# Squares added up on POOL, ScalarE or VectorE, spreads by transposes, two partial sums in layer 1, in a decoder trunk of two layers

## The chip, the core and the metric

The kernel runs on one core of one Trainium2 chip. The metric is the time of one execution on the device, in microseconds (us). The core's engines are TensorE (PE in the rows, its weight loads PEld), VectorE (DVE), ScalarE (ACT), GpSimd (POOL) and SyncE (SP), which here issues nearly all DMAs. Each engine works through its own queue in order.

## What is computed

```python
for l in range(DEPTH):                       # 2 layers, 256 tokens, 1024 channels, float32
    h = rmsnorm(x, norm_mix[l])
    (u_ssm, q_lat, kv_lat, k_rope, hg_q, hg_f, hg_i, hg_g, gate_logits) = jnp.split(h @ w_in[l], split_at, axis=-1)
    y_ssm = s5_mixer(u_ssm, ...)             # diagonal complex recurrence
    y_mla = mla_mixer(q_lat, kv_lat, k_rope, ...)   # rmsnorm of q_lat and kv_lat, 8 heads
    y_hg = hgrn2_mixer(hg_q, hg_f, hg_i, hg_g, ...) # gated linear recurrence, rmsnorm of each head
    merged = gates[:, :, 0] * y_ssm + gates[:, :, 1] * y_mla + gates[:, :, 2] * y_hg
    x = x + merged @ w_out[l]
    x = x + memory_cross_attention(rmsnorm(x, norm_cross[l]), rmsnorm(mem, norm_mem[l]), ...)
    x = x + swiglu_ffn(rmsnorm(x, norm_ffn[l]), ffn_w_gate_up[l], ffn_w_down[l])
return rmsnorm(x, norm_final)
```

Every rmsnorm needs the mean of the squares of a token's channels.

## The kernel before

Activations lie with channels on the partitions: x is four tiles xp of 128 partitions by 2 channel blocks by 256 tokens. Weights are loaded by SP in chunks of 1 MB (tile raw, three buffers), and ACT and DVE split each of a chunk's two halves (a unit) into a high part wH and a low part wL in the reduced float32 format fp32r; the normalised operand x is split in the same way into a pair. A product is then three matmuls, high with high, high with low, low with high. `mm3` (L403) makes them in one of two forms. With 256 columns of output these are three matmuls of 256 columns that all add into one half of a PSUM bank. With 512 columns one matmul multiplies the high weights with both parts of x at once, which gives two partial sums side by side in one bank, and a second one of 256 columns adds the third product; someone must then add the two partial sums:

```python
if o.shape[1] == 512:
    mm(o, w[0], x.rearrange("p s t -> p (s t)"), start=first, stop=False)
    mm(o[:, 256:512], w[1], x[:, 0], start=False, stop=last)
```

`pair` (L420) projects 256 output channels into one bank by the first form, `halves` (L427) into two banks by the second, `quad` (L434) 512 channels into four banks by either, and `add_up` (L447) adds two partial sums, by a copy on ACT and an add on DVE for each bank. In both layers the cross attention and the feed-forward part (tiles hv, quad, fa, fu) use the second form. The first projections of a layer (u by `quad`; hf, hq, hg, ql and kv by `pair`) use the first form; their PSUM tiles are named quad, hf and acc.

**Norms.** `Norm.add` squares x by ACT and adds the four squares on DVE to one tile acc of 2 blocks by 256 tokens. `col_sums` (L563) sums that over the partitions on PE: for each half of the tokens (tt_) and each block one matmul of the squares (as the weights) with a column of ones, into a tile ms. A float32 matmul stands as two instructions in the rows. In layer 0's first norm each of the four squares is summed so on its own, by `first` (L624), between the matmuls of u. `mem_norm` (L1129) does the same for the memory, and the tile lat holds the sums for the norms of q_lat and kv_lat. POOL takes the power -1/2 (`rsqrt`, L239). `row_of` (L613) spreads the resulting column, one number per token, over all partitions: a matmul of the broadcast column with the unit matrix `ident`, then a copy by ACT (tiles R, Rkv, Rm). `hgrn` (L962) spreads its eight columns into tiles ro in the same way.

**What sets the order.** The program is written as one main sequence (the projections) and tasks (generators: the recurrences s5 and hgrn, the attention, the memory), of which `pace` (L262) runs a step whenever the planner's own clocks say that DVE and ACT have room. `step` (L250) marks a task as not to be taken up again before its operations are done by these clocks plus a gap, `LATS`, one number per layer. Then a scheduler with a model of the engines orders each engine's queue; `high_priority` moves a piece ahead. `Plan` (L105) gives each tile a buffer of its kind (t4 of 16 KB, t2, t1 and smaller) from a first pass over the program.

In the s5 task (`s5_main`, two halves per layer) PE transposes Gp into PSUM tiles gt, ACT copies these to G, PE makes tm, then b from G, DVE and POOL run the recurrence, PE makes y, SP moves the result ysh by 16 small DMAs into yc, ACT and DVE split it into yx, which is the operand of the last branch (zg, zo). The attention task makes S, PT and oT; mo and ho project the other two branches. A name gt stands for the gates' matmuls as well (with wH and wL).

## Time and profile before

| what | value |
|---|---|
| three runs | 1100.15, 1101.13, 1104.74 us; median 1101.13 |
| the profiled execution | 1100.18 us, of which span 1098.4 us |
| PE busy | 1083.1 us, 6704 matmuls |
| DVE, ACT, POOL busy | 821.5, 641.1, 23.9 us |
| mean granted clock of PE | 0.994 |
| read from memory | 173 MB |

The profile is of one execution. The span runs from its first to its last instruction, and the run's time holds some 1.8 us more around it. A busy time is the sum of an engine's instructions. Matmuls are pipelined, so the duration of one is longer than the distance to the next start. A wait stands for the idle time of an engine just before an instruction, with what ended it.

### The profile page before, as it was taken

To read this page: it belongs to the slowest core of one execution; us is meant where nothing else is said; L and a number is where in the kernel's file an instruction comes from. 1 tells how busy PE (TensorE), PEld (TensorE's weight loads), DVE (VectorE), ACT (ScalarE), POOL (GpSimd) and SP (SyncE) were. 2 spreads that over 40 slices of the span, in tenths; PEclk is the share of its full clock that TensorE was granted. 3 is DMA by queue.
4 is the path that set the end of the run, shared out by engine and by line. 5 is a ranking of instruction groups with operands and counts; after the bars stand their busy time and mean duration, and the time that the engine had idled before them with its cause. 6 is when DMAs were issued, how large, how long until landed. Compare 5 with 4: busy or idle time off the path is not lost.

```text
span 1098.4 us, 17246 instructions
## 1 busy us (share of the span) xinstructions
PE 1083.1 (99%) x6704; PEld 960.9 (87%) x6704; DVE 821.5 (75%) x1415; ACT 641.1 (58%) x1050; POOL 23.9 (2%) x44
## 2 busy tenths in 40 slices
PE   9999999999999999999999999999999999999997
PEld 9999888887788888888899999888878888888887
DVE  7996877587586799986767877658677767877653
ACT  6647565954456566555555348775555566655552
POOL 1000000000000000000000001000000000000000
PEclk9999999999999999999999999999999999999999
DMA  9735523323644465655655443434474534655561
GB/s 312 214 110 183 175 96 120 123 93 112 223 154 154 154 197 178 198 183 169 206 176 150 123 133 125 154 115 153 133 241 154 192 115 155 206 182 186 173 199 50
DMA packets 146306, 177.69 MB, mean 162 GB/s; under 512 B 15153, under 2 KB 110385, under 8 KB 146225
## 3 DMA queue, kind: packets, MB, share of 16 engines
q1 hardware_dynamic: 145792, 176.03, 49.9%
q8 instruction: 52, 0.85, 0.3%
q10 hardware_dynamic: 432, 0.57, 0.2%
q14 instruction: 30, 0.24, 0.1%
HBM read 173.43 MB, written 1.05 MB: 159 GB/s over the span
## 4 chain that ended last, share of the span: by engine, by line
PE 92%; ACT 3%; DVE 1%; DMA 1%; issue 1%; SPq 0%; POOLq 0%; POOL 0%; ACTq 0%; DVEq 0%
PE hv L204 27%; PE dn L204 11%; PE gt L204 11%; PE acc L204 8%; PE quad L204 7%; PE vps L204 2%; PE lv L204 2%; PE mo L204 2%; PE xv L204 2%; PE y L204 2%; PE zg L204 2%; PE hf L204 2%; PE zo L204 2%; PE b L204 1%; PE q L204 1%; ACT wH L223 1%
## 5 line engine op out<-in xcount | busy, mean ns | idle before, releaser
L223 ACT ACTIVATE wH<-raw 128x1024 fp32r<-128x1024 f32 (+2 forms) x332 | 341.2, 1032 | 318.4 <-PE hv L204 66.9
L212 DVE TENSOR_TENSOR wL<-raw,wH 128x1024 fp32r<-128x1024 f32 (+2 forms) x332 | 393.7, 1189 | 172.2 <-ACT wH L223 167.6
L204 PE MATMUL hv<-h,wH 128*128 128x512 f32 x704 | 247.0, 396 | 0.0
L204 PE MATMUL hv<-h,wL 128*128 128x256 f32 x704 | 195.9, 281 | 0.0
L204 PEld LDWEIGHTS hv<-h,wH 128*128 128x128 f32 x704 | 131.4, 188 | 30.5
L204 PEld LDWEIGHTS hv<-h,wL 128*128 128x128 f32 x704 | 132.9, 189 | 0.9
L204 PE MATMUL gt<-wH,h 128*128 128x512 f32 x384 | 123.9, 402 | 0.0
L204 PE MATMUL acc<-h,wH 128*128 128x256 f32 x480 | 88.8, 285 | 0.0
L204 PEld LDWEIGHTS gt<-wH,h 128*128 128x128 f32 x384 | 70.5, 189 | 13.3
L204 PE MATMUL gt<-wL,h 128*128 128x512 f32 x192 | 75.6, 395 | 0.0
L204 PEld LDWEIGHTS acc<-h,wH 128*128 128x128 f32 x480 | 75.0, 191 | 0.4
L204 PE MATMUL acc<-h,wL 128*128 128x256 f32 x240 | 68.0, 283 | 0.0
L204 PE MATMUL dn<-dx,wH 128*128 128x512 f32 x176 | 61.8, 394 | 0.0
L204 PE MATMUL dn<-wH,dx 128*128 128x256 f32 (+1 forms) x264 | 58.8, 319 | 0.0
L204 PE MATMUL dn<-dx,wL 128*128 128x256 f32 x176 | 49.4, 281 | 0.0
L204 PEld LDWEIGHTS dn<-wH,dx 128*128 128x128 f32 x264 | 43.6, 189 | 4.0
L204 PEld LDWEIGHTS acc<-h,wL 128*128 128x128 f32 x240 | 45.9, 191 | 0.0
L204 PE MATMUL quad<-h,wH 128*128 128x256 f32 (+1 forms) x192 | 45.4, 323 | 0.2 <-ACT wH L223 0.2
L204 PEld LDWEIGHTS gt<-wL,h 128*128 128x128 f32 x192 | 36.0, 188 | 7.6
L204 PE MATMUL dn<-wL,dx 128*128 128x256 f32 (+1 forms) x132 | 41.9, 319 | 0.0
L204 PEld LDWEIGHTS dn<-dx,wH 128*128 128x128 f32 x176 | 33.1, 188 | 7.8
L204 PEld LDWEIGHTS quad<-h,wH 128*128 128x128 f32 x192 | 30.9, 190 | 3.2 <-ACT wH L223 0.5
(362 smaller groups left out, 2093.7 us busy)
## 6 DMA issues: line engine op xcount, KB each, us to landing
raw<-in_w_in_dram SPq DMA_DIRECT2D x48, 1024.0 KB, 5.2
raw<-in_ffn_w_gate_up_dram SPq DMA_DIRECT2D x40, 1024.0 KB, 5.1
raw<-in_ffn_w_down_dram SPq DMA_DIRECT2D x17, 1024.0 KB, 5.2
raw<-in_ssm_w_glu_dram SPq DMA_DIRECT2D x16, 512.0 KB, 4.3
raw<-in_w_out_dram SPq DMA_DIRECT2D x8, 1024.0 KB, 7.3
raw<-in_x_w_kv_dram SPq DMA_DIRECT2D x8, 1024.0 KB, 5.2
raw<-in_ffn_w_down_dram SPq DMA_DIRECT2D x6, 768.0 KB, 4.5
raw<-in_hg_w_o_dram SPq DMA_DIRECT2D x4, 1024.0 KB, 5.0
```

The source lines that it names most:

```text
L204: return PE.matmul(o, l, r, start=start, stop=stop)
L212: DVE.tensor_tensor(out=o, in0=a, in1=b, op=op)
L223: return ACT.activation(out=o, in_=a, func=f, **kw)
```

## The change

1. The squares are added up before PE sums them. `fold` adds the two channel blocks of a square, on DVE or POOL, and `col_sums` is left with one matmul for each half of the tokens. In layer 0's first norm POOL adds the four squares as they come and folds the result, and PE sums once. For q_lat the add of two squares moves from DVE to POOL, with the fold.
2. The memory's norm is taken from a second copy of the memory with tokens on the partitions (`mem_rows`, 1 MB more to load), by two ACT squares that also accumulate; `mem_norm` and its sums on PE are gone.
3. `wide_col` spreads a column by a PE transpose in place of a float32 matmul, in `row_of` and for ro.
4. In layer 1 u, hf, hq, hg, ql and kv are made as two partial sums (`halves`, and `quad` with n=512) and added by `add_up`.
5. The planner: `LATS` (0.9, 1.7) in place of (1.1, 2.2); a task can ask for more time at a yield (2.0 us after the move to yc, 1.5 us after the power function in hgrn); small tiles may take a larger buffer where their kind is full.

The diff, with unchanged lines left out:

```diff
--- before
+++ after
@@ -80,6 +80,7 @@
         o[n] = c(v[n].reshape(T, KD, 128).transpose(2, 1, 0))
+    o["mem_rows"] = v["mem"].reshape(T, DM)
     o["gains"] = c(np.concatenate([v[n].reshape(-1, 128) for n, _ in GAINS]).T)
@@ -96,7 +97,7 @@
 LEAD = 2
-LATS = (1.1,2.2)
+LATS = (0.9, 1.7)
 WIDE = 2
@@ -121,17 +122,21 @@
-                e = ends[kind]
-                h = min(range(len(e)), key=lambda q: e[q])
-                if e[h] >= first:
-                    raise MemoryError(f"no home for tile {i}, {kind}")
-                e[h] = last
-                self.homes[i] = h
+
+                for k in dict(t1=("t1", "t2", "t4"), t2=("t2", "t4")).get(kind, (kind,)):
+                    e = ends[k]
+                    h = min(range(len(e)), key=lambda q: e[q])
+                    if e[h] < first:
+                        e[h] = last
+                        self.homes[i] = f"{k}_{h}"
+                        break
+                else:
+                    raise MemoryError(f"no home for tile {i}, {kind}, at {first}")
...
-        t_ = pool.tile(shape, dt, tag=f"{kind}_{i if self.homes is None else self.homes[i]}", name=name)
+        t_ = pool.tile(shape, dt, tag=self.homes[i] if self.homes else f"{kind}_{i}", name=name)
@@ -249,14 +254,16 @@
 
+
         was = dict(now)
+        more = 0.0
         try:
-            next(e[0])
+            more = next(e[0]) or 0.0
         except StopIteration:
...
         if moved:
-            e[1] = max(moved + [now["pe"]]) + gap_[0]
+            e[1] = max(moved + [now["pe"]]) + gap_[0] + more
         return bool(moved)
@@ -560,17 +567,19 @@
 
-    def col_sums(sqs, ps=None, first=True, last=True, pin=False):
+    def fold(s, E=None):
+
+        if E is not None:
+            E.tensor_tensor(out=s[:, 0], in0=s[:, 0], in1=s[:, 1], op=ALU.add)
+        else:
+            tt(s[:, 0], s[:, 0], s[:, 1], ALU.add)
+        return s[:, 0]
+
+    def col_sums(s, ps=None):
 
         ps = ps if ps is not None else bank("ms")[:, 0:2]
-        for n, s in enumerate(sqs):
-            for tt_ in range(2):
-                for o in range(2):
-
-                    m = mm(ps[:, tt_:tt_ + 1], s[:, o, tt_ * 128:tt_ * 128 + 128], ones,
-                           start=first and n + o + tt_ == 0, stop=last and n == len(sqs) - 1 and o + tt_ == 2)
-                    if pin:
-                        tc.keep_in_program_order(m)
+        for tt_ in range(2):
+            mm(ps[:, tt_:tt_ + 1], s[:, tt_ * 128:tt_ * 128 + 128], ones)
         return ps
@@ -603,19 +612,24 @@
             if self.sums is None:
-                self.sums = col_sums([self.acc])
+                self.sums = col_sums(fold(self.acc))
             ms = tk([2])
...
 
+    def wide_col(o, col):
+
+        now["pe"] += 0.11
+        PE.transpose(o, col.to_broadcast([128, 128]), ident)
+
     def row_of(col, o):
...
             for tt_ in range(2):
-                mm(ps[:, tt_ * 128:(tt_ + 1) * 128], col[:, tt_:tt_ + 1].to_broadcast([128, 128]), ident)
+                wide_col(ps[:, tt_ * 128:(tt_ + 1) * 128], col[:, tt_:tt_ + 1])
             acopy(o, ps[:, 0:256])
@@ -637,8 +651,10 @@
             sq0.append(s)
-        if k > 3:
-            nrm.sums = col_sums(sq0[k - 4:k - 3], nrm.sums, k == 4, k == 7, True)
+            if j:
+                POOL.tensor_tensor(out=sq0[0], in0=sq0[0], in1=s, op=ALU.add)
+            if j == 3:
+                fold(sq0[0], POOL)
 
@@ -948,7 +964,7 @@
                     SP.dma_start(out=yc[32 * c_:32 * c_ + 32, :, j, :], in_=ysh[32 * j:32 * j + 32, c_::4, :])
-            yield
+            yield 2.0
             yx = t4([2, 2, 256], F32R, "yx")
@@ -1045,14 +1061,14 @@
         rsqrt(ro, mo)
-        yield
+        yield 1.5
         for hp in range(2):
...
                     c_ = 2 * (2 * hp + o) + tt_
-                    mm(rp[:, 256 * o + 128 * tt_:256 * o + 128 * tt_ + 128], ro[:, c_:c_ + 1].to_broadcast([128, 128]), ident)
+                    wide_col(rp[:, 256 * o + 128 * tt_:256 * o + 128 * tt_ + 128], ro[:, c_:c_ + 1])
             ov = osb[:, 2 * hp:2 * hp + 2]
@@ -1124,18 +1140,16 @@
             memT.extend(m4[:, j] for j in range(2))
+        nat = [t4([1024], F32, "mnat") for _ in range(2)]
+        for tt_ in range(2):
+            SP.dma_start(out=nat[tt_], in_=A["mem_rows"][128 * tt_:128 * tt_ + 128])
         yield
 
-    def mem_norm():
-
-        ps = None
-        for j in range(4):
-            s = t2([2, 256], F32, "sqm")
-            act(s, memT[j], AF.Square)
-            ps = col_sums([s], ps, j == 0, j == 3)
-            yield
-        ms = tn([2])
-        ts(ms, ps, 1.0 / DM, EPS, ALU.mult, ALU.add)
+        junk, msq, ms = t4([1024], F32, "junk"), tn([2]), tn([2])
+        for tt_ in range(2):
+            act(junk, nat[tt_], AF.Square, accum_out=msq[:, tt_:tt_ + 1])
+            yield
+        ts(ms, msq, 1.0 / DM, EPS, ALU.mult, ALU.add)
         rsqrt(rmc, ms)
@@ -1148,8 +1162,6 @@
             yield
-        if l == 0:
-            yield from mem_norm()
 
@@ -1170,12 +1182,36 @@
         Ue = t4([4, 4, 64], F32, "Ue")
-        qp = quad(C["u"], hx, first if l == 0 else None)
+        wider = l > 0
+
+        def scaled(a, c):
+
+            if wider:
+                add_up(a, halves(c, hx))
+                tt(a, a, Rp, ALU.mult)
+            else:
+                tt(a, pair(c, hx), Rp, ALU.mult)
+
+        def two_tiles(c):
+            if not wider:
+                return pair(c, hx)
+            a = t2([2, 256], F32, "lt")
+            add_up(a, halves(c, hx))
+            return a
+
+        qp = quad(C["u"], hx, first if l == 0 else None, 512 if wider else 256)
+        if l == 0:
+            nrm.sums = col_sums(sq0[0][:, 0])
         ms, r = nrm.finish()
...
         with tc.high_priority(offset=HP):
+            if wider:
+                us = [t2([2, 256], F32, "us") for _ in range(2)]
+                for q in range(2):
+                    add_up(us[q], qp[2 * q:2 * q + 2])
+                qp = [us[o // 2][:, o % 2] for o in range(4)]
             for o in range(4):
@@ -1191,18 +1227,16 @@
         for i in range(2):
-            ps = pair(C["hf"][i], hx, ps=mbank("hf") if i < (2, 1)[l] else None)
             a = t2([2, 256], F32, "a")
-            tt(a, ps, Rp, ALU.mult)
+            scaled(a, C["hf"][i])
             act(a, a, AF.Tanh, scale=0.5)
...
         for i in range(2):
-            ps = pair(C["hq"][i], hx)
             a, tq = t2([2, 256], F32, "a"), t2([2, 256], F32, "tq")
-            tt(a, ps, Rp, ALU.mult)
+            scaled(a, C["hq"][i])
             act(tq, a, AF.Tanh, scale=0.5)
@@ -1216,9 +1250,8 @@
         for i in range(2):
-            ps = pair(C["hg"][i], hx)
             a, tq = t2([2, 256], F32, "a"), t2([2, 256], F32, "tq")
-            tt(a, ps, Rp, ALU.mult)
+            scaled(a, C["hg"][i])
             act(tq, a, AF.Tanh, scale=0.5)
@@ -1226,7 +1259,7 @@
         for i in range(2):
-            ps = pair(C["ql"][i], hx)
+            ps = two_tiles(C["ql"][i])
             s = t2([2, 256], F32, "sqq")
@@ -1235,8 +1268,9 @@
                 split_g(qx[:, o, 0], qx[:, o, 1], ps[:, o], gain("mla_q_norm", 4 * l + k))
-        tt(sq2[0], sq2[0], sq2[1], ALU.add)
-        ps = pair(C["kv"], hx)
+        POOL.tensor_tensor(out=sq2[0], in0=sq2[0], in1=sq2[1], op=ALU.add)
+        fold(sq2[0], POOL)
+        ps = two_tiles(C["kv"])
         skv = t2([2, 256], F32, "skv")
@@ -1256,10 +1290,9 @@
         lps = sbank("lat")
+        fold(skv)
         for n, s in ((0, sq2[0]), (1, skv)):
-            for tt_ in range(2):
-                for o in range(2):
-                    mm(lps[:, 2 * n + tt_:2 * n + tt_ + 1], s[:, o, tt_ * 128:tt_ * 128 + 128], ones, start=o == 0, stop=o == 1)
+            col_sums(s[:, 0], lps[:, 2 * n:2 * n + 2])
         me, lat, rl = tn([2]), tn([4]), tn([4])
```

The sequence on the engines changes with it. Three places, as the queues stand before and after; a number behind a name is the tile's, and the rows of the changed kernel have the line numbers of its own file.

PE in layer 0's first stage, where quad is the projection u, h the operand, ms the sums and row the spread. Before, near the end of the sums (four are in the row, each two instructions):

```order
L204 MATMUL quad_135<-h_115,wL_170 128x256
L204 MATMUL ms_247<-ones,sq_268 128x1 x4
L204 MATMUL quad_132<-h_116,wH_175 128x256 x2
L204 MATMUL quad_132<-h_116,wL_176 128x256
L204 MATMUL quad_133<-h_116,wH_175 128x256 x2
```

and with the change:

```order
L209 MATMUL quad_135<-h_116,wH_175 128x256 x2
L209 MATMUL ms_317<-ones,sq_193 128x1 x2
L209 MATMUL quad_132<-h_116,wL_176 128x256
L209 MATMUL quad_133<-h_116,wL_176 128x256
L209 MATMUL quad_134<-h_116,wL_176 128x256
```

Four rows of sums between the matmuls of u became one, 80 matmuls into u, and the fifth row block of u follows the fourth directly.

POOL from the start of the program, where A and Vp are tiles of zeros, n is the norm's power function and rh half of it. Before:

```order
L1295 MEMSET Vp_1322 128x1024
L241 ISA
L241 TENSOR_TENSOR n_332<-n_330,mhalf 128x2
L1213 TENSOR_SCALAR rh_716<-n_332 128x2
L862 MEMSET rt_1756 128x8
```

and with the change:

```order
L1328 MEMSET Vp_1305 128x1024
L655 ISA
L655 TENSOR_TENSOR sq_193<-sq_193,sq_229 128x512
L655 TENSOR_TENSOR sq_193<-sq_193,sq_264 128x512
L655 TENSOR_TENSOR sq_193<-sq_193,sq_301 128x512
L573 TENSOR_TENSOR sq_193<-sq_193 128x256
L246 TENSOR_TENSOR n_322<-n_320,mhalf 128x2
```

Three adds and the fold stand ahead of the power function that the first spread needs.

PE at the second half of layer 0's s5 task. Before:

```order
L869 MATMUL gt_2384<-ident,Gp_2285 128x128 x4
L869 MATMUL gt_2356<-ident,Gp_2284 128x128 x4
L204 MATMUL tm_2424<-Pw_961,Gp_2284 32x64
...
L204 MATMUL S_2694<-Kh_1312,Qh_1310 128x256
L204 MATMUL b_2462<-Ush_343,G_2348 128x64 x4
L204 MATMUL b_2463<-Ush_343,G_2349 128x64 x4
L1071 MATMUL PT_2449<-ident,Ssb_2296 128x128 x3
```

and with the change:

```order
L885 MATMUL gt_2429<-ident,Gp_2330 128x128 x4
L209 MATMUL tm_2465<-Pw_1097,Gp_2330 32x64
...
L209 MATMUL S_2490<-Kh_1295,Qh_1293 128x256
L209 MATMUL gt_2415<-wH_2318,h_113 128x512 x2
L209 MATMUL gt_2415<-wL_2319,h_113 128x512
L209 MATMUL b_2510<-Ush_333,G_2388 128x64 x8
L209 MATMUL b_2511<-Ush_333,G_2389 128x64 x8
```

One group of transposes is left in front of tm; three gate matmuls stand between S and b, and all eight of the first b come ahead of the second. Some way behind, 12 matmuls of mo stand ahead of y's main group, where 7 stood before.

## Rows read from the trace of the kernel before

**Rows 1.** The page's busy times: us (share of span) xinstructions.

```profile
PE 1083.1 (99%) x6704; PEld 960.9 (87%) x6704; DVE 821.5 (75%) x1415; ACT 641.1 (58%) x1050; POOL 23.9 (2%) x44
```

**Rows 2.** Waits of PE: tile <- what it waited for: us, times, longest.

```profile
PE mT L1375 <- DVE Tg L212: 1.9, 1, 1.9
PE mo L204 <- ACT Tg L223: 1.2, 1, 1.2
PE b L204 <- ACT G L223: 1.2, 1, 1.2
PE zg L204 <- DVE yx L212: 0.9, 1, 0.9
```

**Rows 3.** Stretches, layer 0: us, PE PEld DVE ACT POOL busy, clock, DMA, GB/s.

```profile
215.00:220.00 5.00, 3.80 (x25) 3.40 (x24) 2.73 (x5) 4.97 (x10) 0.00 (x0) 0.82 0.75 256
220.00:225.00 5.00, 5.00 (x24) 4.82 (x24) 4.57 (x11) 3.63 (x10) 0.11 (x1) 0.50 0.75 272
286.00:290.00 4.00, 3.19 (x12) 2.86 (x13) 3.84 (x7) 0.00 (x0) 0.00 (x0) 0.57 0.37 123
```

**Rows 4.** Chain that ended last, first 60 us: start us, us, what.

```profile
6.81 6.01 PE quad L204 x48
12.82 0.79 PE ms L204 x8
...
24.16 0.45 PE row L204 x4
...
34.09 11.52 PE acc L204 x96
```

**Rows 5.** Chain that ended last: two later pieces.

```profile
390.61 104.18 PE hv L204 x597
...
685.95 1.78 PE ro L204 x16
```

**Rows 6.** Groups by line, PE: shapes | busy us, mean ns | idle before.

```profile
L204 PE MATMUL ms<-ones,sq 128*128 128x1 f32 x72 | 8.5, 240 | 0.0
...
L204 PE MATMUL ms<-ones,sqm 128*128 128x1 f32 x32 | 3.7, 245 | 0.0
...
L204 PE MATMUL row<-ident,n 128*128 128x128 f32 x16 | 2.4, 274 | 0.0
...
L204 PE MATMUL lat<-ones,skv 128*128 128x1 f32 x16 | 1.9, 239 | 0.0
```

**Rows 7.** Timeline of PE at transposes: start us, us, instructions.

```profile
211.82 1.04 PE L869 MATMUL gt<-ident,Gp 128*128 128x128 f32 x8
212.78 1.97 PE L204 MATMUL tm<-Pw,Gp 128*32 128x64 f32 x32
```

**Rows 8.** Groups by line, PE: transposes of one kind.

```profile
L869 PE MATMUL gt<-ident,Gp 128*128 128x128 f32 x64 | 8.6, 272 | 0.0
```

**Rows 9.** Groups by line, ACT and DVE, in the feed-forward part.

```profile
L223 ACT ACTIVATE fa<-hv 128x256 f32<-128x256 f32 x40 | 14.6, 366 | 0.0
...
L212 DVE TENSOR_TENSOR fa<-fa,hv 128x256 f32<-128x256 f32 x40 | 16.5, 413 | 0.0
```

**Rows 10.** Stretches of layer 1's projections and of the feed-forward part.

```profile
570.00:590.00 20.00, 20.00 (x186) 19.78 (x186) 12.09 (x18) 14.73 (x22) 0.72 (x2) 1.00 0.40 101
600.00:610.00 10.00, 10.00 (x49) 8.39 (x49) 10.00 (x15) 4.49 (x5) 0.11 (x1) 1.00 0.55 173
400.00:450.00 50.00, 50.00 (x287) 43.59 (x287) 48.85 (x90) 30.89 (x50) 0.00 (x0) 1.00 0.59 195
```

**Rows 11.** Timeline of ACT in the first stage.

```profile
12.19 2.18 ACT L223 ACTIVATE wH<-raw 128x512 fp32r<-128x512 f32 x4
```

**Rows 12.** Timeline of POOL.

```profile
0.76 0.95 POOL L966 MEMSET A<- 128x1024 f32 x1
...
171.38 1.64 POOL L241 TENSOR_TENSOR s<-s,mhalf 128x8 f32<-128x8 f32 x1 [5.43 <-DVE s L219]
```

**Rows 13.** Timeline of PE before the last branch of layer 0.

```profile
265.53 0.50 PE L204 MATMUL zg<-wH,yx 128*128 128x512 f32 x1 [0.90 <-DVE yx L212]
```

## The prediction, made before the run

> **What bounds the kernel now.** I read the engines' busy shares first [rows 1]: TensorE (PE) is busy for 1083.1 of the 1098.4 us of the span, VectorE (DVE) and ScalarE (ACT) for three quarters and for less than two thirds. A busy PE can be a PE that idles inside long matmuls, so I read next what PE waited for [rows 2]: its four longest waits are of 1.9, 1.2, 1.2 and 0.9 us, all in layer 0 between 215 and 287 us, and they are nearly all that there is once the matmuls have begun. Then the granted clock of that stretch [rows 3]: after the wait of 1.2 us at 215 us the clock is at its lower level (1.2 in place of 2.4 GHz) for 36% of 215 to 220 us and all of 220 to 225, and after the wait of 1.9 us at 285 us for 86% of 286 to 290; at the lower level work takes twice as long, so these cost 0.9 + 2.5 + 1.7 = 5.1 us. Waits and clock together are 5.2 + 5.1 = 10.3 us. Everywhere else matmul follows matmul. So the kernel is bound by the number of matmuls times the distance from one start to the next, and this distance, not the duration of one matmul, is the price of everything that the change takes from PE. Distances I take from the chain that ended last, where PE's pieces follow each other without a gap [rows 4, 5].
>
> **The sums on PE.** A float32 matmul stands as two instructions in the rows. Column sums (tiles ms and lat) are 72 + 32 + 16 + 16 instructions [rows 6] (lat has two groups alike, one of which stands there). After the change layer 0's first norm keeps 4 of its 32, the five other norms keep 4 of 8 each, the memory's 32 go altogether, lat keeps 16 of 32: 24 + 0 + 16 = 40 are left, 96 go. Eight of them take 0.79 us in the chain [rows 4], 0.099 us each: **-9.5 us**.
>
> **The spreads.** A column is spread by 64 matmul instructions now: 16 in row for the norms [rows 6] and two rows of 8 like it, 16 in ro in each layer [rows 5]. Four take 0.45 us [rows 4], sixteen 1.78 us [rows 5], so 0.112 us each, 7.2 us together. A transpose of 128x128 is one instruction: eight follow each other from 211.82 us until the next group starts at 212.78 [rows 7], 0.12 us each. 32 of them cost 3.8 us: **-3.3 us** (the two ends of the new price are 0.12, the distance, and 0.272, the duration of one [rows 8], as if none overlapped; I take 0.12, since PE does start the next one that soon). TensorE: Matmul & The Clock Gate in the Trainium skill (Part 4: PE-mode transpose) gives about 275 ns for a transpose in a kernel's context; the duration in the trace agrees, the distance does not, and by the page's price this term would be +1.6 us in place of -3.3.
>
> **The second layer's projections.** As one sum a 256-column chunk is 48 matmuls of 256 columns; 96 take 11.52 us [rows 4], 0.120 each, 5.76 a chunk. As two sums it is 16 of 512 and 16 of 256; 597 such take 104.18 us [rows 5], 0.1745 each, 5.58 a chunk. Nine chunks save 0.18 each, the u projection (96 to 64 matmuls) 11.52 - 11.17 = 0.35: **-1.9 us**.
>
> **What the other engines get.** Each of the nine pairs, and u as two more, gains two ACT copies of 256 columns and two DVE adds (0.366 and 0.413 us) [rows 9], the multiplication by R staying one of 512: 22 of each, 8.1 us of ACT and 9.1 of DVE, over the 90 us of layer 1's projections. I cost it at nothing: from 400 to 450 us, where all chunks are made this way, DVE is busy 48.85 of 50 us and PE never idles [rows 10]. The cover is thinner from 600 to 610 us, where DVE already is busy 10.00 of 10 us with the recurrence's steps [rows 10]; that is the first rival. Seven halving adds of 256 columns come to DVE (five norms, lat's second sum in each layer), 0.4 us each: PE's sums stand behind them in its queue, but only after many more matmuls of the projection under way than these 0.4 us. In return the add of the two lat squares leaves DVE for POOL, which is nearly idle. The memory's rows, 1 MB more to load, go out on SP ahead of the last branch's weights; SP has no other load to make there, since each of these waits for a raw buffer, and ACT's squares of them take the place of four others.
>
> **POOL in the first stage.** The new order puts the two sums after 80 matmuls of u, and PE works in order, so a late POOL stops PE there. PE starts at 6.81 us and reaches that place at 6.81 + 80 x 0.12 = 16.4 us. The last square is done when ACT turns to its four weight pieces at 12.19 us [rows 11]. Behind it stand one POOL add of 512 and one of 256 columns. The trace has no such add. From below: a POOL memset of 1024 columns takes 0.95 us [rows 12], 0.48 for 512, as if reading were free. From above: the power function on 8 columns takes 1.64 us [rows 12], 0.2 us a column, 105 us for 512. I take 1.4 us (two reads and a write, each as dear as the memset's write), far nearer to the memset, since an add is no power function; 1.5 x 1.4 = 2.1 us end at 14.3 us, 2 us before PE asks. GPSIMD Engine Reference in the Trainium skill (4.1 Engine selection) says to leave two-input elementwise work to VectorE, being about twice as slow on POOL, and its 4497 ns for 2048 columns make an estimate of 1.1 us; the sum would be the same. What PE meets there instead: with no sums between, it wants the weights of the fifth row block at 6.81 + 48 x 0.12 = 12.6 us, and ACT has the first piece (a quarter of 2.18 us [rows 11]) at 12.75: +0.2 us.
>
> **The moved waits.** Before b (layer 0, second half) PE sends both its last groups of transposes, tm and S, then waits 1.2 us for ACT's copies [rows 2]. In the new order one group goes far earlier, and between the last and the first b that needs it stand gate matmuls and 8 of b: -1.2 us. Before the second zg group PE waits 0.9 us for yx, behind the move of y through SP [rows 13]; now 12 in place of 7 mo matmuls stand ahead of y, so 5 of 512 columns fewer lie behind it, at (5.58 - 16 x 0.12) / 16 = 0.23 us from the chunk above: +1.2 us. The two that remain, mo and mT, I leave as they are; the shorter gap of the planner (0.9 and 1.7 us) can move them either way.
>
> Sum: -9.5 - 3.3 - 1.9 = -14.7; + 0.2 - 1.2 + 1.2 = **-14.5 us**. The profiled execution took 1100.2 us, 0.9 under the median of the three runs and beside their fastest. **1085.7 us**.
>
> **Rivals.**
> 1. DVE becomes the bound in layer 1's projections. For it: 10.00 of 10 us at 600 us. Against: from 570 to 590 us, where u and both hf pairs fall (four of the eleven), DVE is busy 12.09 of 20 us [rows 10] and takes its share. If all that is added for the other seven came back as waits, 14 x 0.413 = 5.8 us: 1091.5.
> 2. In-order waits take over, and it gets slower. With gaps of 1.1 us layer 0 has its four waits, each with its share of the lower clock 10.3 / 4 = 2.6 us; layer 1, with 2.2, has none. The change shortens both gaps and speeds PE up against DVE and ACT. If layer 0 gets four more and layer 1 as many as that, +20.6 us: 1106.3. It decides from six such waits on (14.5 / 2.6). Against: the special waits behind the SP move and the power function, and the order, in which the producers of layer 1 stand well ahead.
> 3. What PE loses was filler: sums and spreads come out, and PE waits that long at the next operand instead; the change then does not do what it says: 1100. Against: no wait of PE stands anywhere near most of these instructions [rows 2].
> 4. A transpose costs its duration: 32 x (0.272 - 0.12) = +4.9, 1090.6. The page named above has that price; the trace speaks against it [rows 7, 8].
> 5. POOL adds at the power function's rate: three and a half adds of 105 us, some 1450. Only the far bound speaks for it.
>
> **Chances.** Forecast 0.70 (its own range 1080 to 1091: the lower clock gone, or two more waits of 2.6 us), rival 1 0.10, rival 2 0.06, rival 3 0.07, rival 4 0.04, rival 5 0.03. A difference of 0.5%, 5.5 us, is what a measurement of this kernel can tell. Faster by more: 0.70 + 0.10 + 0.04 = 0.84; within: 0.07; slower: 0.06 + 0.03 = 0.09. The range reaches down to 1078 (the 5.1 us of lower clock gone, and mT's wait of 1.9 too: 1078.7) and up to 1094, past rivals 1 and 4.
>
> **What would show it.** PE matmul instructions fall by 96 + 32 + 9 x 16 + 32 = 304, from 6704 to 6400. First stage: sums at about 16.4 us without a wait, the first pair of projections at 6.81 + 96 x 0.12 + 0.4 + 0.2 = 18.9 us. Row and ro groups at half their length. Layer 1: 32 matmuls a chunk in 5.6 us, and DVE above nine tenths from 590 us on without waits of PE. A wait for POOL at the first sums, waits on DVE in layer 1's hv, or the clock at its lower level in layer 1 would make the prediction wrong.

## The result, and the profile of the changed kernel

The changed kernel took 1095.62 us (median of nine runs, 1093.08 to 1099.84). The kernel before took 1104.74 us in nine runs beside them. The ratio is 0.9932 with a 95% interval of 0.9911 to 0.9952: faster by 0.7%, half of what was forecast, and outside the range of 1078 to 1094. The profiled execution took 1093.08 us, its span 1091.3. It is the fastest of the nine; its mean granted clock is 0.994, as in the profiled execution before, so the two profiles can be compared: 7.1 us lie between their spans, 9.1 between the medians, 14.5 in the forecast.

The page's busy times of the changed kernel, beside [rows 1]:

```profile
PE 1067.1 (98%) x6400; PEld 934.5 (86%) x6400; DVE 831.5 (76%) x1442; ACT 649.6 (60%) x1074; POOL 39.9 (4%) x52
```

PE has the 6400 matmuls that were forecast, and is busy 16.0 us less; the forecast had 14.7. But the span is only 7.1 us shorter, so 8.9 us of that went into idle time. The view of PE's waits names it (tile, what it waited for, us in total, times, longest), beside [rows 2]:

```profile
PE oT L209 <- ACT PT L228: 4.4, 2, 3.8
PE quad L209 <- DVE m L217: 3.1, 3, 1.7
PE zg L209 <- ACT yx L228: 2.9, 1, 2.9
PE quad L209 <- DVE wL L217: 2.3, 2, 2.1
PE S L209 <- DVE mox L217: 1.2, 1, 1.2
```

All lines of this view come to 17.7 us, those of before to 8.0. The waits of b for G and of mo and mT for Tg, which stood before, are gone; these five are new or longer, and but for 0.3 us of the waits for m, there before as well, all of them are in layer 0. From the first matmul on u to layer 1's first, PE took 549.5 us before and 551.1 now; layer 1 took 534.9 and now 526.5. So layer 1 gave the whole gain, and layer 0 lost 1.6 us with 92 matmuls fewer.

The clock, in stretches of 5 us (columns as in [rows 3]), falls to its lower level at two of these waits, those for PT and for yx, which end at 220.26 and 270.17 us; 5.1 us are lost by it in all, as much as before:

```profile
220.00:225.00 5.00, 4.74 (x31) 4.22 (x31) 1.23 (x1) 2.98 (x5) 0.00 (x0) 0.66 0.38 119
270.00:275.00 5.00, 4.83 (x11) 3.80 (x12) 2.83 (x4) 2.68 (x4) 0.00 (x0) 0.50 0.87 299
```

The first stage shows the first loss. The timelines of POOL and DVE (start, us, instructions):

```profile
8.85 1.59 POOL L655 TENSOR_TENSOR sq<-sq,sq 128x512 f32<-128x512 f32 x1 [5.33 <-ACT sq L228]
10.77 1.46 POOL L655 TENSOR_TENSOR sq<-sq,sq 128x512 f32<-128x512 f32 x1 [0.33 <-ACT sq L228]
...
14.24 1.21 POOL L573 TENSOR_TENSOR sq<-sq 128x256 f32<-128x256 f32 x1
```

```profile
9.18 1.28 DVE L217 TENSOR_TENSOR s<-s 128x4 f32<-128x4 f32 x1
10.38 0.68 DVE L217 TENSOR_TENSOR wL<-raw,wH 128x512 fp32r<-128x512 f32 x1
10.98 1.26 DVE L217 TENSOR_TENSOR s<-s,s 128x4 f32<-128x4 f32 x1
...
12.96 1.30 DVE L224 TENSOR_SCALAR hb<-s 128x4 f32<-128x4 f32 x2
14.17 0.68 DVE L217 TENSOR_TENSOR wL<-raw,wH 128x512 fp32r<-128x512 f32 x1
```

The same places of DVE's queue before:

```profile
9.00 0.16 DVE L212 TENSOR_TENSOR s<-s 128x4 f32<-128x4 f32 x1
...
10.63 0.23 DVE L219 TENSOR_SCALAR hb<-s 128x4 f32<-128x4 f32 x2
10.99 0.69 DVE L212 TENSOR_TENSOR wL<-raw,wH 128x512 fp32r<-128x512 f32 x1
```

An operation on 4 columns, which takes 0.15 to 0.16 us elsewhere in this stage, takes 1.28 and 1.26 us: it starts beside a POOL add and ends just when the add does (8.85 + 1.59 = 10.44, 9.18 + 1.28 = 10.46). The third stop, 1.30 us for two operations that took 0.23, is of operations with one tensor as input. Behind the three, wL of the fourth row block comes at 14.17 + 0.68 us, in place of 10.99 + 0.69, and PE, which wanted it from 12.8 on, waits:

```profile
14.91 0.75 PE L209 MATMUL quad<-h,wL 128*128 128x256 f32 x4 [2.10 <-DVE wL L217]
...
19.76 0.50 PE L209 MATMUL ms<-ones,sq 128*128 128x1 f32 x4
```

The sums themselves come at 19.76 us, 4.3 us after POOL's fold is done (14.24 + 1.21). So POOL was in time, as forecast, and what it did to DVE was not in the forecast. u takes 15.0 us from its first matmul to its last, before as now.

### The profile page after: what moved, and what is told of

Same layout as the page of the kernel before. It is cut to its first block, busy times and chain, and to the rows that moved or that the text cites. A ratio compares the mean times of both kernels' runs of the same rounds, so it can differ in the third digit from the quotient of the medians.

```text
span 1091.3 us, 16705 instructions
## 1 busy us (share of the span) xinstructions
PE 1067.1 (98%) x6400; PEld 934.5 (86%) x6400; DVE 831.5 (76%) x1442; ACT 649.6 (60%) x1074; POOL 39.9 (4%) x52
## 4 chain that ended last, share of the span: by engine, by line
PE 71%; ACT 1%; DVE 0%; issue 0%; POOLq 0%; POOL 0%; ACTq 0%
PE hv L209 32%; PE dn L209 11%; PE quad L209 6%; PE gt L209 6%; PE xv L209 2%; PE ho L209 1%; PE mo L209 1%; PE zg L209 1%; PE vps L209 1%; PE y L209 1%; PE lv L209 1%; PE zo L209 1%; PE xo L209 1%; PE b L209 1%; PE xS L209 1%; PE q L209 1%
## 5 line engine op out<-in xcount | busy, mean ns | idle before, releaser
L209 PE MATMUL hv<-h,wH 128*128 128x512 f32 x848 | 298.2, 396 | 0.0
L209 PE MATMUL hv<-h,wL 128*128 128x256 f32 x848 | 235.7, 280 | 0.0
L209 PEld LDWEIGHTS hv<-h,wH 128*128 128x128 f32 x848 | 158.6, 188 | 36.0
L209 PEld LDWEIGHTS hv<-h,wL 128*128 128x128 f32 x848 | 159.8, 188 | 0.9
L209 PEld LDWEIGHTS gt<-wH,h 128*128 128x128 f32 x384 | 71.0, 189 | 13.8
L209 PE MATMUL acc<-h,wH 128*128 128x256 f32 x288 | 52.5, 284 | 0.0
L209 PEld LDWEIGHTS acc<-h,wH 128*128 128x128 f32 x288 | 44.9, 192 | 0.1
L209 PE MATMUL quad<-h,wH 128*128 128x512 f32 (+1 forms) x160 | 43.3, 351 | 0.4 <-ACT wH L228 0.4
L209 PE MATMUL acc<-h,wL 128*128 128x256 f32 x144 | 40.8, 284 | 0.2 <-DVE wL L217 0.2
L209 PE MATMUL quad<-h,wL 128*128 128x256 f32 x128 | 32.6, 285 | 2.3 <-DVE wL L217 2.3
L209 PEld LDWEIGHTS dn<-dx,wL 128*128 128x128 f32 x176 | 33.0, 187 | 0.0
```

Source lines behind the costliest of these rows:

```text
L209: return PE.matmul(o, l, r, start=start, stop=stop)
```

## The experiments

Each run's span is split in three: **waits** (all lines of the view of PE's waits), **lower clock** (in stretches of 5 us up to 1060 us, 5 us times what the granted clock lacks to 1), and **the rest**, which is PE's work. The sum is good to some 2 us. The profile is of one execution, the slowest of its run for first_old and the fastest for the change. Medians are of each run's own executions; the ratio is to the runs of before beside it, whose medians go from 1099.8 to 1105.1 us, so that a step of 0.004 between two ratios can come from before alone.

| run | median us | ratio, 95% interval | waits | lower clock | rest |
|---|---|---|---|---|---|
| before | 1104.74 | | 8.0 | 5.1 | 1085.3 |
| the change | 1095.62 | 0.9932, 0.9911 to 0.9952 | 17.7 | 5.1 | 1068.4 |
| b_pool | 1108.28 | 1.0062, 1.0031 to 1.0092 | 10.8 | 13.6 | 1084.5 |
| no_add | 1091.40 | 0.9892, 0.9852 to 0.9931 | 18.1 | 6.8 | 1066.5 |
| pool_memset | 1093.48 | 0.9909, 0.9876 to 0.9941 | 16.6 | 6.8 | 1066.3 |
| dve_add | 1097.19 | 0.9953, 0.9932 to 0.9975 | 13.9 | 18.9 | 1065.3 |
| first_old | 1086.15 | 0.9850, 0.9820 to 0.9881 | 9.9 | 10.3 | 1068.8 |
| narrow1 | 1097.49 | 0.9978, 0.9963 to 0.9992 | 18.8 | 8.5 | 1068.4 |
| no_sin | 1093.35 | 0.9926, 0.9902 to 0.9950 | 15.9 | 10.2 | 1067.4 |
| ny | 1094.41 | 0.9921, 0.9894 to 0.9948 | 15.8 | 8.5 | 1067.1 |
| mem_old | 1100.98 | 0.9972, 0.9958 to 0.9986 | 19.9 | 10.2 | 1069.7 |
| gaps_back | 1115.23 | 1.0128, 1.0099 to 1.0156 | 27.8 | 22.1 | 1065.4 |
| heads1 | 1095.28 | 0.9917, 0.9893 to 0.9940 | 13.5 | 12.0 | 1066.5 |
| heads4 | 1093.32 | 0.9898, 0.9875 to 0.9922 | 16.4 | 3.4 | 1069.9 |
| dve_heads1 | 1091.82 | 0.9895, 0.9866 to 0.9924 | 11.6 | 10.3 | 1067.0 |
| first_lat10 | 1086.14 | 0.9851, 0.9814 to 0.9888 | 10.4 | 3.4 | 1069.0 |
| first_lat08 | 1089.96 | 0.9883, 0.9848 to 0.9917 | 11.9 | 8.5 | 1067.1 |
| first_heads1 | 1084.75 | 0.9825, 0.9799 to 0.9851 | 8.6 | 8.5 | 1068.4 |
| fh1_lat10 | 1084.97 | 0.9843, 0.9803 to 0.9882 | 9.3 | 3.4 | 1069.4 |
| fh1_ychalf | 1085.44 | 0.9858, 0.9818 to 0.9897 | 9.2 | 3.4 | 1069.0 |

### The first stage: does POOL stop DVE?

**b_pool**, before with three adds that nobody uses:

```diff
+            if j:
+                POOL.tensor_tensor(out=spare[0], in0=sq0[0], in1=s, op=ALU.add)
```

> The kernel before, with three POOL adds of 512 columns on the squares of the first stage whose result nobody uses; PE, ACT, DVE and SP keep their instructions and their order. If a POOL add keeps DVE's two-input operations waiting (lock theory): beside each add a DVE operation of 128x4 columns lasts 1.2 to 1.3 us in place of 0.16, wL comes 1 us or more later, PE waits for wL by 1.5 to 2.5 us in the first stage, and the whole is 1.5 to 3 us longer (ratio 1.001 to 1.003). If the long DVE operations of the changed kernel come from its own order or from the loads that fill the memory there: DVE's operations keep 0.16 us, no wait over 0.3 us in the first stage, ratio 1.000.

The wait came out as the lock theory had it, and the time by more. DVE and PE in the same places:

```profile
8.92 1.27 DVE L212 TENSOR_TENSOR s<-s 128x4 f32<-128x4 f32 x1
```

```profile
14.64 0.74 PE L204 MATMUL quad<-h,wL 128*128 128x256 f32 x4 [2.09 <-DVE wL L212]
```

```profile
15.00:20.00 5.00, 5.00 (x34) 5.00 (x33) 4.90 (x13) 2.73 (x4) 0.00 (x0) 0.69 1.07 366
20.00:25.00 5.00, 5.00 (x25) 5.00 (x25) 1.73 (x6) 1.06 (x1) 0.00 (x0) 0.50 1.10 349
```

Three instructions on the idlest engine, with every other queue as it was, cost 6.8 us (0.62% of 1101). In the profile u takes 22.3 us in place of 15.0: 2.1 us of wait, and behind it some 5 us of lower clock. That second part was missed by all theories. In the profile of the changed kernel the clock held behind the same wait, and so it did in no_sin and heads4; in the profiles of ny, heads1, narrow1, mem_old and gaps_back, whose first stage is alike, it fell (0.66 to 0.68 from 15 to 20 us).

**no_add** takes POOL's part away from the changed kernel (only the first square is summed), **pool_memset** lets POOL write in place of adding:

```diff
-                POOL.tensor_tensor(out=sq0[0], in0=sq0[0], in1=s, op=ALU.add)
+                POOL.memset(sq0[0], 1.0)
```

> The changed kernel without the three POOL adds and the fold of the first stage: its first norm sums one square alone, the other three are left out. The queues keep their order but for some 25 rows. If the lock in the first stage costs the changed kernel its 2.3 us and in some executions the lower clock behind it: DVE's operations of 128x4 last 0.16 us, no wait for wL over 0.4 us, u takes 12.2 to 12.8 us in place of 15.0, the waits from 205 to 300 us stay as they are, 1090 to 1093 us. If all that the run with the first sums on PE won (some 9 us) came from the first stage: 1086 to 1088. If the loads that fill the memory there set the end of u: 15 us as before, and 1095.

> The changed kernel with a POOL memset of the same 512 columns in place of each of the three adds: POOL writes and reads nothing (the squares are left out of the norm). If any work of POOL on the memory stops DVE: operations of DVE beside a memset are stretched by up to its 0.5 us, u takes 13 to 14 us. If it is POOL's reading that stops DVE's second operand: DVE's operations keep their durations, u 12.2 to 12.8 us, 1090 to 1093 us, as without the adds; the fold, which reads, may still stretch one.

Without the adds u takes 12.0 us in place of 15.0, and no wait for wL is left there. With memsets it takes 12.2. POOL and DVE of pool_memset:

```profile
5.51 1.69 POOL L655 MEMSET sq<- 128x512 f32 x3 [1.99 <-ACT sq L228]
7.28 0.91 POOL L573 TENSOR_TENSOR sq<-sq 128x256 f32<-128x256 f32 x1
```

```profile
6.90 0.69 DVE L217 TENSOR_TENSOR wL<-raw,wH 128x512 fp32r<-128x512 f32 x1
7.51 0.17 DVE L675 RECIPROCAL s<-s 128x4 f32<-128x4 f32 x1
7.60 1.14 DVE L217 TENSOR_TENSOR wL<-raw,wH 128x512 fp32r<-128x512 f32 x1
```

Beside the memsets wL has its 0.69 us; beside the fold, which reads, the next one takes 1.14 in place of 0.66 (no_add). So it is POOL's reading that stops DVE. The Trainium skill says the same on its page SBUF — State Buffer (Who interferes with whom): DVE and POOL share a pair of ports as an exclusive lock, and a DVE instruction with two inputs in SBUF contends with a POOL instruction that reads, not with one that only writes. The traces agree, with 1.27 us for an operation of 0.16; the third stop above, of operations with one input, is no case of two inputs. I had not weighed this rule in the prediction.

Yet the 3 us did not reach the end in the profiled run of no_add: the last branch (zo) ends 4.8 us earlier than in the change, and the feed-forward part at the same time, since PE then waits 3.3 us for m and the clock falls there. In the medians no_add is 4 us faster than the change and pool_memset 2, with intervals that overlap.

**dve_add** puts the adds on DVE (`tt(sq0[0], sq0[0], s, ALU.add)`, `fold(sq0[0])`), **first_old** puts the sums of the four squares on PE again, as in [rows 4]:

> The changed kernel with the three adds and the fold of the first stage on DVE in place of POOL: 3 x 0.68 and 0.41 us more on DVE, no lock. If the lock was the cost: u takes 12.4 to 13.2 us in place of 15.0. If DVE, busy 5.94 of 6 us there, was the limit anyway: each add delays wL by its 0.68 us, u takes 14 to 15 us, and the place of the adds did not matter. The order of the rest of layer 0 changes as well.

> The changed kernel with layer 0's first sums on PE again (32 instructions in place of 4), and no POOL adds there. By the forecast's sum 28 instructions come back, +2.8 us. By the lock theory POOL's adds cost PE as much as they saved: u takes the same 15.0 us from its first to its last matmul, the wait of 2.1 us for wL is gone, and with it the risk of the lower clock behind it; the first stage itself is worth 0 to -0.5 us. The order of the rest of layer 0 is another one, which by itself may give some us either way; with the waits from 205 to 300 us as they are, 1093 to 1096 us.

On DVE the adds let u end after 12.8 us, the shortest of the three places that still do the work (PE and POOL: 15.0). The lock theory held, and the total did not profit: further on this version lost 18.9 us to the lower clock. first_old's u takes 15.0 us, as its expectation said, and has no wait; but the whole is 9 us faster than the change, which no term for the first stage can give. Its waits are 9.9 us in place of 17.7. From u's first matmul on, 2.6 us of waits less lie ahead of 205 us, and 6.4 less from 205 to 300 us, where nothing was edited; ahead of u PE waits 1.1 us longer.

### Layer 1

**narrow1** sets `wider = False`: layer 1's first projections as one sum.

> The changed kernel with layer 1's first projections as one sum (three matmuls of 256 columns), as before. Layer 0 is to be as in the changed kernel, with its waits. By the forecast's sum layer 1 is 1.9 us longer; by the traces of before and of the change, whose projections and feed-forward part on h differ by 3.7 us in layer 1, up to 3.7; if DVE's adds held PE up in layer 1 (rival 1) it is not longer at all.

Layer 1 took 528.5 us in place of 526.5: 2.0 us for the 176 matmuls, against 1.9 in the forecast. Rival 1 falls with it; in the change PE is busy throughout while DVE is at nine tenths:

```profile
600.00:650.00 50.00, 50.00 (x319) 44.99 (x319) 45.70 (x73) 22.88 (x35) 0.23 (x2) 1.00 0.37 115
```

### Layer 0's waits

**no_sin** replaces the sine and cosine of one half by `AF.Identity`, so that ACT's table loads fall away and no queue moves:

```diff
+            wave = AF.Identity if (l, hf) == (0, 1) else AF.Sin
-            act(sn, y, AF.Sin, scale=SIN_SCALE)
+            act(sn, y, wave, scale=SIN_SCALE)
```

> The changed kernel, in which the second half of layer 0's recurrence takes its two angles as they are and leaves out the sine and cosine of them; every queue keeps its order, and only four loads of ACT's function table (1.28 us each) fall away between 209 and 219 us. If the order is to blame, by these loads: the wait of 3.8 us for PT at 216 us shrinks under 0.5 us, the lower clock behind it (0.66 from 220 to 225 us) goes, G comes earlier, and with it b, y and yx: 4 to 8 us less than the changed kernel, some 1088 to 1091 us. If the recurrence's own chain through DVE and SP sets the end of layer 0 and PE only lost filler: the wait moves to zg or b, and 0 to 2 us are won.

ACT's timeline in the change, ahead of the wait for PT, and PE's wait:

```profile
209.17 1.28 ACT L228 ACT_TABLE_LOAD   x1
...
212.38 1.28 ACT L228 ACT_TABLE_LOAD   x1
213.67 0.69 ACT L228 ACTIVATE Tg<-gt,rh 128x512 f32<-128x512 f32 x1
214.38 1.28 ACT L228 ACT_TABLE_LOAD   x1
215.67 0.72 ACT L228 ACTIVATE cs<-ph,cf 128x512 f32<-128x512 f32 x1
216.30 1.04 ACT L228 ACTIVATE wH<-raw 128x1024 fp32r<-128x1024 f32 x1
217.36 1.28 ACT L228 ACT_TABLE_LOAD   x1
...
219.72 0.49 ACT L228 ACTIVATE PT<-PT 128x384 f32<-128x384 f32 x1
```

```profile
220.26 0.92 PE L209 MATMUL oT<-PT,Vp 128*128 128x256 f32 x4 [3.83 <-ACT PT L228]
```

In no_sin:

```profile
214.35 0.49 ACT L228 ACTIVATE PT<-PT 128x384 f32<-128x384 f32 x1
```

```profile
PE quad L209 <- DVE m L217: 4.5, 3, 2.5
PE zg L209 <- ACT yx L228: 2.9, 1, 2.9
...
PE S L209 <- DVE mox L217: 1.7, 1, 1.7
```

The new order put a sine, a tanh, a cosine and a tanh behind one another on ACT, each with a table load of 1.28 us (15 in all, 13 before). Without them PT is copied 5.4 us earlier and the wait is gone; PE is 5.1 us ahead when it comes to b. The whole wins 2.3 us by the medians, with intervals that overlap: in the profile the time comes back as waits for mox and m and as lower clock (10.2 us in place of 5.1). The cause of this one wait is shown; removing it did not make the kernel faster by its length.

**ny** takes the two longer yields away (`yield` in place of `yield 2.0` and `yield 1.5`), **gaps_back** also sets `LATS = (1.1, 2.2)`; **mem_old** makes the memory's norm by 32 sums on PE again:

> The changed kernel without the extra time at the two yields (2.0 and 1.5 us), with its gaps of 0.9 and 1.7. ACT loads its function table twice, not four times, around 210 us. If the table loads alone were the cost: as the run without the sine, no gain at the end, 1093 to 1096 us. If the yields put the tasks in a bad order: 1088 to 1091. If they were there to keep PE from waiting: the wait at ro or at zg grows past 3 us, 1097 to 1103.

> The changed kernel with the planner's numbers of before: gaps of 1.1 and 2.2 us, no extra time at the two yields. If the planner's numbers cost layer 0 its gain: its waits and its lower clock from 205 to 300 us fall from some 16 us to about the 10 of before, 1088 to 1091 us. If they don't (filler theory, or an order that any edit shuffles anew): waits of like sum at other places, 1093 to 1098 us.

> The changed kernel with the memory's norm made from squares of its transposed copy by 32 matmul instructions again, and no second copy loaded. By the forecast's sum +3.2 us (32 x 0.099). If the 32 sums were cover for the waits before quad (m, 1.3 and 1.8 us) that PE now sits through: 0 to +1 us. If the extra load and ACT's two squares of 1.05 us delayed layer 0's last steps: less than the changed kernel by 1 to 3 us.

ny is where the change is. gaps_back is the surprise: with the planner's old numbers the changed kernel is slower than the one before by 1.3%, with 27.8 us of waits and 22.1 of lower clock, in layer 1 too (clock 0.62 at 840 us). Its longest:

```profile
PE mT L1408 <- DVE Tg L217: 5.8, 2, 3.3
PE ro L625 <- POOL s L246: 3.6, 1, 3.6
PE mo L209 <- DVE Ssb L217: 3.2, 1, 3.2
```

Since ny is where the change is, it is the gaps and not the yields: the shorter gaps carry the change, not its loss. mem_old gave PE 32 instructions back (3.4 us), its waits grew to 19.9 us, and by the medians it is 5.4 us slower, above the 3.2 of the forecast's sum: these sums were no cover, which speaks against rival 3.

**first_lat10** and **first_lat08** change one number of first_old, layer 0's gap (1.0 and 0.8 in place of 0.9):

> The run with the first sums on PE (1086.2 us), with the planner's gap of layer 0 at 1.0 us in place of 0.9: the same work, some 290 rows of PE's queue in other places. If layer 0's waits hang on the particular order of its queues: 3 us or more from that run, either way. If they follow the gap smoothly: within 1.5 us of it.

> The same with the gap at 0.8 us. By the order theory again 3 us or more from 1086.2 us either way, and not the mirror image of the run with 1.0; by the smooth one within 1.5 us, on the other side of it than the run with 1.0.

1.0 gives the same median, 0.8 is 3.8 us slower, with intervals that overlap. By the medians neither theory is clearly right. The sums of waits and lower clock in the three profiles are 20.2, 13.8 and 20.4 us, and the waits alone 9.9, 10.4 and 11.9: what differs most is the lower clock.

**heads1** and **heads4** let the second half of layer 0's recurrence start after one or four heads (`HEADS`). They tested a theory formed on the way: in all fourteen kernels until then the feed-forward part of layer 0 ended 306 to 312 us after y's last matmul.

> The changed kernel, in which the second half of layer 0's recurrence may start after one head of the attention in place of three (the work is the same). In the runs so far layer 0's feed-forward part ends 306 to 312 us after the last matmul of y, which came between 232 and 259 us. If the date of y sets the end of layer 0 (chain theory): y ends some 5 us earlier, and the end of layer 0 and the whole with it, 1088 to 1092 us, though not one matmul is gone. If PE's waits hang on the order alone: no such tie, anything from 1088 to 1104. If PE's work is the bound: no change, 1094 to 1096.

> The same with four heads in place of three. By the chain theory y ends later, by about 8 us of PE's work, and the whole takes 4 to 8 us more than the changed kernel, 1099 to 1104 us. If PE's work is the bound: 1094 to 1096.

It fell. In heads1 y ended 8.2 us earlier (235.9 us after the first matmul on u, in place of 244.1) and the feed-forward part at 550.8 in place of 551.0. In heads4 y ended 3.0 us later and that part 2.3 us earlier. The likeness of the fourteen was no cause.

### The end of layer 0's mixers, and a better version

**dve_heads1** and **first_heads1** are dve_add and first_old with one head; **fh1_lat10** is first_heads1 with the gap at 1.0; **fh1_ychalf** is first_heads1 with

```diff
-                    SP.dma_start(out=yc[32 * c_:32 * c_ + 32, :, j, :], ...
+                    (SP if c_ % 2 else POOL).dma_start(out=yc[32 * c_:32 * c_ + 32, :, j, :], ...
```

> One head, and the adds of the first stage on DVE in place of POOL. By the lock theory u takes 12.8 us, by the chain theory the earlier start is passed on to y: the run with the adds on DVE had y's end at 248 us, here its place in PE's queue is 7.5 us of work earlier. 1082 to 1088 us. If the first stage's gain is again lost before y: 1088 to 1094.

> One head, and the first sums on PE. y's end stands 10 us of PE's work earlier than in the run with the first sums on PE (1086.2 us, where y ended at 236.2 us). By the chain theory 1078 to 1084 us, until PE's work is the bound again (the work left after the waits and the lower clock are taken out is some 1070 us); if y's date no longer decides below 236 us: 1085 to 1087.

> The run with one head and the first sums on PE (1084.8 us), with half of y's 16 small copies issued by POOL in place of SP; in layer 0 the queues of PE, ACT and DVE keep their order but for a handful of rows. SP needs 10.2 us for the 16 there, and the loads of the weights for the last branch and the output projection stand behind them. If SP's queue sets the end of layer 0's mixers: yx and the loads come up to 5 us earlier, the waits for Tg and m (3.0 and 1.8 us) and the lower clock behind them shrink, 1079 to 1083 us. If the loads wait for the raw buffers that PE's own matmuls free (w_out is issued 18 us after the last copy): yx earlier, the rest as it was, 1083 to 1087. If POOL issues copies much slower than SP: a wait for yx appears, 1086 to 1092.

> The same run with layer 0's gap at 1.0 us in place of 0.9. Work and first stage are the same. By the order theory another sum of waits and lower clock, somewhere in the 14 to 19 us that the three best runs had: 1081 to 1088 us.

dve_heads1 came out at 1091.8 us, in the range that its expectation had for a gain lost again before y. But y ended 229.1 us after the first matmul on u, in place of heads1's 235.9 and dve_add's 248.0: the gain stood at y, and half of it was lost behind y (zo 2.7 us earlier than in heads1, the feed-forward part 3.4). The other expectations: first_heads1 at 1084.8, between its two ranges; fh1_lat10 and fh1_ychalf within theirs. In first_heads1 and fh1_ychalf the loads on SP's queue:

```profile
238.54 10.18 SPq L969 DMA_DIRECT2D yc<-ysh  x16
248.82 16.19 SPq L387 DMA_DIRECT2D raw<-in_ssm_w_glu_dram  x6
266.98 11.46 SPq L387 DMA_DIRECT2D raw<-in_w_out_dram  x4
```

```profile
235.00 5.08 SPq L969 DMA_DIRECT2D yc<-ysh  x8
240.18 21.59 SPq L387 DMA_DIRECT2D raw<-in_ssm_w_glu_dram  x6
263.74 11.03 SPq L387 DMA_DIRECT2D raw<-in_w_out_dram  x4
```

Halving the copies frees SP 5 us earlier, and the loads of w_out start 23.6 us after the last copy in place of 18.3. The waits for Tg and m stay (2.5 and 1.5 us, 3.0 and 1.8 before). From y's last matmul to zo's last it takes 48.8 us in the one and 48.9 in the other. So SP's queue is not what holds the end of the mixers. That the loads wait for the raw buffers is argued from this, not shown.

**first_heads1**, 1084.75 us and 0.9825 of before, beats both kernels; first_old, first_lat10, fh1_lat10 and fh1_ychalf can't be told from it. All have the first sums on PE and the rest of the change.

## Why the prediction was wrong

**The terms of PE's work were right.** Summed from start to start over each group, the sums on PE became 10.1 us shorter (forecast 9.5), the spreads 3.7 (3.3), and the second layer's projections 2.0 (1.9). The rest column has 16.9 us. A transposed spread costs 0.07 us in the row tiles and 0.10 in ro, start to start, below the 0.12 that I took and far from its duration of 0.272: rival 4 falls.

**The step that failed is the one on waits.** It stood in two places. "POOL in the first stage" gave +0.2 us. Its price for an add (1.4 us) was right, at 1.46 to 1.59, and so was its question whether POOL is late for PE. What failed is that I looked for the cost only there: the cost was on DVE, 2.1 us of PE's wait, and u with the work done on DVE ends 2.2 us earlier. "The moved waits" gave -1.2 + 1.2 and left mo and mT as they were. The wait for G did go, mo's and mT's also went, and yx's grew by 2.0 us where I had 1.2. But PT (4.4), m (2.6 more) and mox (1.2) came in their place. All waits together rose by 9.7 us, against +0.2 for both terms in my sum; 16.9 us of work less and 9.7 of waits more, at the same lower clock, are the 7.1 us by which the span fell (to rounding).

**Rival 2 came nearest, at a lesser size.** In-order waits took 9.7 us in layer 0, none more in layer 1, and no more lower clock in the profiled execution; it would have needed 14.5 us to turn the sign. gaps_back, with other gaps than the change, shows it in full: slower, with waits and lower clock in layer 1 too. My chance for it was 0.06, and I had priced it as all or nothing, where half of its 20.6 us came. The order that I quoted ahead of the prediction showed that PE's and POOL's queues would be shuffled. ACT's queue, of which I quoted nothing, holds two table loads more than before, and no term of the sum had them.

**What decides the size.** Across the eighteen versions of the change, whose work on PE differs by some 3 us at most, the rest is 1065 to 1070 us, while waits and lower clock together go from 12.6 (fh1_ychalf) to 49.9 us (gaps_back). Two of the waits have a shown cause (POOL's reading, the table loads). Removing one of them brings waits elsewhere in the profile, and edits that touch no matmul move the sum by 10 us and more (dve_add 10, gaps_back 27). That the order of the in-order queues decides, not one engine's bound, is argued from what these runs have in common, and not shown by itself; which feature of first_old's order makes it good is open. That the work taken from layer 0 was filler (rival 3) does not fit: fh1_lat10 and fh1_ychalf have 64 matmuls less there than before, and layer 0 takes 540.2 us in place of 549.5. Open too is why layer 0 lost 1.6 us, where its terms (9.9 us less) and its waits (9.5 more from u's first matmul on) leave a gain of 0.4, and why layer 1 gained 8.4 us where the terms give 5.9: matmuls that were not edited come closer there (the feed-forward part's 512-column ones 236 to 232 ns apart in narrow1).

**The clock taken out.** The results list the mean granted clock of every execution, to a thousandth (1.1 us). Time times clock is from 1092 to 1096 us in all 56 executions of before beside the experiments, whose times go from 1098 to 1107.5. Its medians are 1093.5 us for before, 1086.9 for the change, 1083.0 for no_sin, 1082.8 for no_add, 1079.5 for dve_add and 1078.5 for first_old. So by this estimate POOL's stops and the four table loads cost the change some 4 us each, near the 3.0 us of u and the 3.8 of the wait that go without them; dve_add is as good as first_old but for the clock; and an order sets two things, PE's waits and how long the clock is down.

## What to carry to other kernels

Work that moves to an idle engine is not free because that engine is in time: look in the trace for operations of its neighbours that last longer beside it, and first of all for two-input DVE operations beside POOL operations that read. Where one engine is busy 99% of the span, cut the profile into its work, its waits and the lower clock behind them: work taken away counts in full only where the queues keep their order, and here a gain of 17 us of work ended between 14 us slower (gaps_back) and 19 us faster than before (first_heads1), by the waits and the clock that came with each order. So give such an edit two or three orders (a planner's gap, another start) before judging it, and put a share of a rival's waits into the forecast, not none (half of rival 2's came here).

## What was not expected of the hardware

A wait of 2.1 us can cost 7: in b_pool the clock was at its lower level (1.2 GHz) from some 17 to 27 us, and u took 7.3 us longer. And it falls without any wait. first_old and first_lat10 run the same matmuls up to 171 us, the last 3 us of them nearly all pieces of 64 columns and sums of 1; then the one has its clock fall and the other does not:

```profile
170.00:175.00 5.00, 5.00 (x32) 5.00 (x31) 0.03 (x1) 0.00 (x0) 1.64 (x1) 0.65 0.66 210
175.00:180.00 5.00, 5.00 (x24) 4.81 (x24) 2.20 (x4) 2.30 (x4) 0.39 (x1) 0.50 0.00 0
```

```profile
170.00:175.00 5.00, 5.00 (x48) 5.00 (x48) 0.75 (x2) 0.45 (x1) 1.47 (x1) 1.00 0.66 210
```

The spread between executions of one kernel goes with this clock: before took 1098.0 to 1101.5 us in the 23 executions at 0.994 to 0.996, and 1102.5 to 1107.5 in the 33 below; the change 1093.1 us at 0.994 and 1099.8 at 0.989. What makes it fall in one execution and not in another of the same kernel is open.
